# One-hot gates in bf16 with the gate cut into three parts, and one gather for both expert tables

## The chip, the cores and the metric

The kernel runs on one core of a Trainium2 chip. Its time is the device time of one execution in microseconds (us); the number given for a kernel is the median of its runs. The core has five instruction streams that run at the same time and wait for each other through semaphores: PE (the matrix engine; its weight loads are listed apart as PEld), DVE (vector), ACT (scalar), POOL (general purpose) and SP, which here only issues DMAs. ACT and POOL issue DMAs as well. Each stream runs its instructions in the order in which they were written into it.

## The reference, cut to what matters

Two layers of a mixer (an S5 state space model beside attention) followed by a PEER expert layer, for 512 tokens of width 1024. The change lies in the expert layer:

```python
def peer_ffn(h, w_q, sub_keys, u_tab, v_tab):        # h: (512, 1024); tables: (16384, 1024)
    q = (h @ w_q).reshape(tokens, 8 heads, 2, 64)
    s1, s2 = q[..., 0] @ sub_keys[:, 0], q[..., 1] @ sub_keys[:, 1]     # 128 keys each
    t1, i1 = top_k(s1, 16);  t2, i2 = top_k(s2, 16)
    best, pos = top_k(t1[:, None] + t2[None, :], 16)                    # 16 experts a head
    idx = (i1 * 128 + i2)[pos];  gate = softmax(best)                   # 128 experts a token
    act = gelu(einsum('tkd,td->tk', u_tab[idx], h))
    return einsum('tk,tkd->td', act * gate, v_tab[idx])
```

## The kernel before, in words

The tokens are four blocks of 128. For blocks 0 to 2 (384 tokens, `NT`) the expert layer is computed densely: every one of the 16384 experts is applied to every token, and a gate that is zero for the experts that were not chosen does the choosing. Block 3 is computed by gathering the rows of its chosen experts. Per layer the work goes through these stages.

**Route** (`route_block`, for blocks 3, 0, 1, 2): the top-k lists, nearly all on DVE. For block 3 it leaves `s.idx` (128 row numbers a token) and `s.gate`. For the others it transposes the two key numbers and the gate of every pick through PE into `idT` (three rows of 384 columns; a column is a token, a partition is one of its 128 picks).

**Gates** (`gates`): for each token a 128 x 128 matrix of gates (first key by second key) is made as a product of two one-hot matrices, one of them scaled by the gate. The 384 tokens go in 48 groups of 8. A group has one DVE compare of the iota row with both key rows (`L875`, tile `t8`), a scaling of the first one-hot by the gate (for two groups of three by 8 small ACT instructions, `L879`; for the third by one DVE product, `L881`; tile `small`), 8 float32 matmuls (`L885`; the trace lists each as two passes with two weight loads), and two evictions by ACT (`L887`) into a staging tile, which goes to DRAM as `gd` once in 4 groups. `t8`, `small` and the staging tile have two buffers each.

**First tables** (`u_stage`): 128 blocks of 128 experts. A block's 512 KB come in by an SP DMA (`raw`), ACT writes a rounded copy `hi` (`L166`), the remainder `lo = raw - hi` (`L167`) is made by POOL for the first 116 blocks (`NAHEAD`), and PE does 24 matmuls of 384 columns (`mm3`, `L201` to `L203`). ACT applies the gelu (`L898`) and the result goes to DRAM (`ad`). These blocks do not depend on the gates, so the scheduler puts them between the route and gate instructions as well: they are what PE does while the others route.

**Second tables** (`v_coef`, `v_block`): for each block DVE multiplies the activations by the gates (`L908`), splits the product (`L911`), and PE does 18 matmuls of 512 columns (`L921`). The last 12 blocks of the first table are done in between.

**Gather for block 3** (`gather_step`, `gather_sum`): 128 steps a layer, spread over the stages above from the route on. Step k issues from POOL's queue two indirect DMAs (`L934`), one row of `peer_u` and one of `peer_v` for each of the 128 tokens, into `ru` and `rv` (3 buffers each), and then sums step k-2: a DVE product with a row sum (`L945`, which waits for `ru`), a gelu on ACT (`L946`), a DVE product of a single column with the gate (`L947`), and a DVE multiply-add of `rv` into the output (`L948`). `issue_after(s.pace)` puts the issue behind POOL's last `lo`.

The order on each engine is set by a scheduler that works with its own estimate of durations when the kernel is built; at run time it is fixed.

## Time and profile before

| | |
|---|---|
| median of three runs | 3300.38 us (3298.41, 3300.38, 3734.48) |
| the profiled execution | 3299.41 us, span of its trace 3297.6 us |
| PE busy | 3074.1 us, 93% of the span |
| DVE busy | 2602.4 us, 79% |
| ACT busy | 1432.4 us, 43% |
| POOL busy | 1589.3 us, 48% |
| mean granted clock of PE | 0.970 |

"Busy" counts the time in which at least one instruction of the engine is listed as running. For PE an instruction's listed duration is longer than its spacing from the next, so a busy PE isn't a full one; and an instruction of DVE or POOL that has started but can't go on is still listed as busy. In time, layer 0's route runs from about 400 to 640 us, its gates from 640 to 893, the rest of its first tables to 1080, and its second tables to 1690; layer 1 has the same stages at 2040 to 2283, 2531, 2700 and 3290 us.

### The profile page before, as it was taken

To read this page: it belongs to the slowest core of one execution; us is meant where nothing else is said; L and a number is where in the kernel's file an instruction comes from. 1 tells how busy PE (TensorE), PEld (TensorE's weight loads), DVE (VectorE), ACT (ScalarE), POOL (GpSimd) and SP (SyncE) were. 2 spreads that over 40 slices of the span, in tenths; PEclk is the share of its full clock that TensorE was granted. 3 is DMA by queue.
4 is the path that set the end of the run, shared out by engine and by line. 5 is a ranking of instruction groups with operands and counts; after the bars stand their busy time and mean duration, and the time that the engine had idled before them with its cause. 6 is when DMAs were issued, how large, how long until landed. Compare 5 with 4: busy or idle time off the path is not lost. (4 is left out here: it accounts for less than half of the span.)

```text
span 3297.6 us, 45399 instructions
## 1 busy us (share of the span) xinstructions
PE 3074.1 (93%) x16178; PEld 2687.6 (82%) x16178; DVE 2602.4 (79%) x4892; ACT 1432.4 (43%) x2574; POOL 1589.3 (48%) x880
## 2 busy tenths in 40 slices
PE   8999987889999998999999999878999999999998
PEld 7757977889999776887889679878898998788887
DVE  7754799988776788898867547999886658888887
ACT  3163333478733343343333533334886333333333
POOL 3000476656688544464420004666766884544452
PEclk9999989999999999999999999889999999999999
DMA  6512376667799988999964123766777898999995
GB/s 187 188 54 64 120 253 206 210 239 268 272 310 309 326 304 288 333 331 330 338 217 121 52 71 123 249 219 196 278 256 279 302 319 315 328 352 341 340 336 213
DMA packets 391604, 811.08 MB, mean 246 GB/s; under 512 B 26928, under 2 KB 232752, under 8 KB 388304
## 3 DMA queue, kind: packets, MB, share of 16 engines
q1 hardware_dynamic: 136608, 326.23, 29.0%
q0 software_dynamic: 73728, 268.47, 23.0%
q10 hardware_dynamic: 181040, 213.48, 19.3%
q8 instruction: 127, 2.08, 0.3%
q14 instruction: 101, 0.83, 0.1%
HBM read 693.19 MB, written 114.82 MB: 245 GB/s over the span
## 5 line engine op out<-in xcount | busy, mean ns | idle before, releaser
L167 POOL TENSOR_TENSOR lo<-raw,hi 128x1024 fp32r<-128x1024 f32 x296 | 792.8, 2686 | 890.7 <-ACT hi L166 828.5
L166 ACT ACTIVATE hi<-raw 128x1024 fp32r<-128x1024 f32 x561 | 591.9, 1057 | 602.0 <-issue 157.6
L921 PE MATMUL pb<-hi,cc 128*128 128x512 f32 x2048 | 608.0, 398 | 17.7 <-DVE cc L911 11.5
L945 DVE SCALAR_TENSOR_TENSOR ru<-ru,hn 128x1024 f32<-128x1024 f32 x256 | 378.1, 1478 | 204.0 <-DMA ru<-in_peer_u_dram,idx 204.0
L921 PEld LDWEIGHTS pb<-hi,cc 128*128 128x128 f32 x2048 | 383.9, 189 | 115.2 <-DVE cc L911 16.6
L934 POOL DMA_INDIRECT rv<-in_peer_v_dram,idx x256 | 369.3, 1442 | 136.8 <-issue 45.4
L167 DVE TENSOR_TENSOR lo<-raw,hi 128x1024 fp32r<-128x1024 f32 x265 | 328.6, 1241 | 127.4 <-ACT hi L166 127.2
L934 POOL DMA_INDIRECT ru<-in_peer_u_dram,idx x256 | 377.7, 1476 | 96.1 <-DVE ru L945 33.9
L948 DVE SCALAR_TENSOR_TENSOR h<-rv,gc,h 128x1024 f32<-128x1024 f32 x256 | 404.4, 1580 | 8.2 <-DMA rv<-in_peer_v_dram,idx 5.9
L203 PE MATMUL pa<-x,lo 128*128 128x384 f32 x1120 | 387.2, 346 | 17.2 <-POOL lo L167 16.6
L201 PE MATMUL pa<-x,hi 128*128 128x384 f32 x1120 | 390.4, 349 | 12.5 <-ACT hi L166 12.5
L202 PE MATMUL pa<-x,hi 128*128 128x384 f32 x1120 | 380.1, 339 | 0.0
L201 PE MATMUL pc<-x,hi 128*128 128x384 f32 x928 | 328.4, 354 | 18.7 <-ACT hi L166 12.9
L203 PE MATMUL pc<-x,lo 128*128 128x384 f32 x928 | 325.5, 351 | 19.7 <-POOL lo L167 19.6
L921 PE MATMUL pb<-lo,cc 128*128 128x512 f32 x1024 | 324.8, 398 | 13.2 <-DVE lo L167 11.4
L921 PE MATMUL pc<-hi,cc 128*128 128x512 f32 x1024 | 323.8, 396 | 0.0
L202 PE MATMUL pc<-x,hi 128*128 128x384 f32 x928 | 320.1, 345 | 0.0
L946 ACT ACTIVATE gc<-gc 128x1 f32<-128x1 f32 x256 | 51.4, 201 | 556.5 <-DVE ru L945 506.2
L875 DVE TENSOR_TENSOR t<-io,idt 128x2048 f32<-128x2048 f32 x96 | 260.2, 2722 | 9.1 <-PE pb L885 9.1
L885 PE MATMUL pb<-small,t 128*128 128x128 f32 x1536 | 222.5, 289 | 34.2 <-ACT small L879 21.8
L910 ACT ACTIVATE cc<-c 128x384 fp32r<-128x384 f32 x256 | 133.1, 520 | 267.7 <-DVE c L908 213.1
L885 PEld LDWEIGHTS pb<-small,t 128*128 128x128 f32 x1536 | 211.6, 198 | 46.1 <-ACT small L879 30.5
(334 smaller groups left out, 5798.7 us busy)
## 6 DMA issues: line engine op xcount, KB each, us to landing
raw<-in_peer_uT_dram SPq DMA_DIRECT2D x256, 512.0 KB
raw<-in_peer_v_dram SPq DMA_DIRECT2D x256, 512.0 KB
gd<-t ACTq DMA_DIRECT2D x24, 2048.0 KB
g<-gd ACTq DMA_DIRECT2D x64, 768.0 KB
ad<-ao ACTq DMA_DIRECT2D x232, 192.0 KB
ar<-ad ACTq DMA_DIRECT2D x58, 768.0 KB
raw<-in_w_in_dram SPq DMA_DIRECT2D x34, 512.0 KB
s5p<-pE ACTq DMA_DIRECT2D x16, 512.0 KB
```

Source lines behind the costliest of these rows:

```text
L166: s.nc.scalar.activation(hi, raw, AF.Copy)
L167: ins = eng.tensor_tensor(lo, raw, hi, op=OP.subtract)
L201: mm(ps, lh, rh, start=start, stop=False)
L202: mm(ps, lh, rl, start=False, stop=False)
L203: mm(ps, ll, rh, start=False, stop=stop)
L875: v.tensor_tensor(oh, s.iota[:, None, None, :].to_broadcast([128, 2, 8, 128]), idT[:, 0:2, t0:t0 + 8, None].to_broadcast([128, 2, 8, 128]) ...
L885: nc.tensor.matmul(p[:, t], oh[:, 1, 4 * f + t], o2[:, 4 * f + t], start=True, stop=True)
L910: on_act = nc.scalar.activation(ch, c[:, 0], AF.Copy)
L921: s.nc.tensor.matmul(s.pv[tb][hf], x[:, sl], y[:, 512 * hf:512 * hf + 512], start=(first and e == 0), stop=(last and e == 2))
L934: nc.gpsimd.indirect_dma_start(out=o, out_offset=None, in_=a[n], in_offset=off)
L945: v.scalar_tensor_tensor(ru, ru, 1.0, s.hn, op0=OP.mult, op1=OP.mult, accum_out=c[:, 0:1])
L948: v.scalar_tensor_tensor(acc, rv, c[:, 2:3], acc, op0=OP.mult, op1=OP.add)
```

## The change

The one-hot matrices become bf16. `idT` is now bf16 with five rows: the two key numbers, and the gate as a sum of three bf16 parts. The 8 tokens of a group are held as 4 pairs with the pair innermost, so that neighbouring elements belong to the two tokens of a pair. DVE does two compares (`L882`) and three products (`L884`) of 1024 elements for each group, ACT no scaling; PE does three bf16 matmuls a token (`L890`), which add up in PSUM, each with a weight load. The eviction (`L892`) writes in runs of four tokens where it wrote element by element with a stride of 32. The rows of both expert tables lie behind one another in one DRAM table `peer_uv` (16384 rows of 2048 a layer): a gather step is one indirect DMA (`L939`) of 128 rows of 8 KB into one tile `ruv` (3 buffers), and the second table's blocks are read as the right halves of its rows. The gate product of a gather step moves from DVE to ACT (`L953`). Line numbers of the changed kernel differ a little: the sums `L945` and `L948` are `L951` and `L954` there.

```diff
@@ -117,7 +116,8 @@
         rel = s.t("rel", [128])
         nc.gpsimd.iota(rel, pattern=[[1, 128]], base=0, channel_multiplier=-1,
                        allow_small_or_imprecise_dtypes=True)
-        s.iota = io
+        s.iota2 = s.t("iota2", [128, 2], BF)
+        nc.vector.tensor_copy(s.iota2, io[:, :, None].to_broadcast([128, 128, 2]))
         s.ident = s.t("ident", [128])
         nc.vector.tensor_scalar(s.ident, rel, 0.0, None, op0=OP.is_equal)
         s.identb = s.t("identb", [128], BF)
@@ -856,7 +857,11 @@
             nc.tensor.transpose(p[:, 256:384], g, s.ident)
             ts = slice(b * 128, b * 128 + 128)
             v.tensor_copy(s.idT[:, 0:2, ts], p[:, 0:256].rearrange("p (a b) -> p a b", a=2))
+            rest = cut(12, 1)
             v.tensor_copy(s.idT[:, 2, ts], p[:, 256:384])
+            v.tensor_tensor(rest, p[:, 256:384], s.idT[:, 2, ts], op=OP.subtract)
+            v.tensor_copy(s.idT[:, 3, ts], rest)
+            v.tensor_tensor(s.idT[:, 4, ts], rest, s.idT[:, 3, ts], op=OP.subtract)
 
     def gates(s):
 
@@ -866,25 +871,26 @@
         idT = s.idT
         for tg in range(NT // 32):
             stg = s.t("t16", [128, 32], bufs=2)
-            gs = idT[:, 2, tg * 32:tg * 32 + 32]
             for e in range(4):
                 t0 = tg * 32 + e * 8
 
-                oh = s.t("t8", [2, 8, 128], bufs=2)
-                o2 = s.t("small", [8, 128], bufs=2)
-                v.tensor_tensor(oh, s.iota[:, None, None, :].to_broadcast([128, 2, 8, 128]),
-                                idT[:, 0:2, t0:t0 + 8, None].to_broadcast([128, 2, 8, 128]), op=OP.is_equal)
-                if GMODE[(4 * tg + e) % len(GMODE)] == "A":
-                    for t in range(8):
-                        nc.scalar.activation(o2[:, t], oh[:, 0, t], AF.Copy, scale=gs[:, 8 * e + t:8 * e + t + 1])
-                else:
-                    v.tensor_tensor(o2, oh[:, 0], gs[:, 8 * e:8 * e + 8, None].to_broadcast([128, 8, 128]), op=OP.mult)
+                oh = s.t("t8", [2, 4, 128, 2], BF, bufs=2)
+                o3 = s.t("small", [3, 4, 128, 2], BF, bufs=2)
+                col = lambda i: idT[:, i, t0:t0 + 8].rearrange("p (a t) -> p a t", t=2)[:, :, None, :] \
+                    .to_broadcast([128, 4, 128, 2])
+                for i in range(2):
+                    v.tensor_tensor(oh[:, i], s.iota2[:, None].to_broadcast([128, 4, 128, 2]), col(i), op=OP.is_equal)
+                for i in range(3):
+                    v.tensor_tensor(o3[:, i], oh[:, 0], col(2 + i), op=OP.mult)
                 for f in range(2):
                     p = s.p("pb").rearrange("p (t i) -> p t i", t=4)
                     for t in range(4):
-                        nc.tensor.matmul(p[:, t], oh[:, 1, 4 * f + t], o2[:, 4 * f + t], start=True, stop=True)
-                    o = stg[:, :, e * 8 + f * 4:e * 8 + f * 4 + 4].rearrange("p i t -> p t i")
-                    nc.scalar.activation(o, p, AF.Copy)
+                        x = 2 * f + t // 2
+                        for i in range(3):
+                            nc.tensor.matmul(p[:, t], oh[:, 1, x, :, t % 2], o3[:, i, x, :, t % 2],
+                                             start=(i == 0), stop=(i == 2))
+                    nc.scalar.activation(stg[:, :, e * 8 + f * 4:e * 8 + f * 4 + 4], p.rearrange("p t i -> p i t"),
+                                         AF.Copy)
             nc.scalar.dma_start(gd[tg], stg)
         s.gd = gd
 
@@ -927,11 +933,10 @@
         k = s.gk
         s.gk += 1
         if k < 128:
-            r = [s.ga.tile([128, D], F32, name=f"{n}{s.l}_{k}", tag=n, bufs=GLAG + 1) for n in ("ru", "rv")]
+            r = s.ga.tile([128, 2 * D], F32, name=f"ruv{s.l}_{k}", tag="ruv", bufs=GLAG + 1)
             off = bass.IndirectOffsetOnAxis(ap=s.idx[:, k:k + 1], axis=0)
             with s.tc.issue_after(getattr(s.pace, "ins", s.pace)):
-                for o, n in zip(r, ("u_flat", "v_flat")):
-                    nc.gpsimd.indirect_dma_start(out=o, out_offset=None, in_=a[n], in_offset=off)
+                nc.gpsimd.indirect_dma_start(out=r, out_offset=None, in_=a["uv_flat"], in_offset=off)
             s.grow[k] = r
         if 0 <= k - GLAG < 128:
             s.gather_sum(k - GLAG)
@@ -939,12 +944,13 @@
     def gather_sum(s, k):
         nc = s.nc
         v = nc.vector
-        ru, rv = s.grow.pop(k)
+        r = s.grow.pop(k)
+        ru, rv = r[:, 0:D], r[:, D:2 * D]
         acc = s.h[:, 3]
         c = s.ga.tile([128, 4], F32, name=f"gc{s.l}_{k}", tag="gc", bufs=4)
         v.scalar_tensor_tensor(ru, ru, 1.0, s.hn, op0=OP.mult, op1=OP.mult, accum_out=c[:, 0:1])
         nc.scalar.activation(c[:, 1:2], c[:, 0:1], AF.Gelu_apprx_tanh)
-        v.tensor_tensor(c[:, 2:3], c[:, 1:2], s.gate[:, k:k + 1], op=OP.mult)
+        nc.scalar.activation(c[:, 2:3], c[:, 1:2], AF.Copy, scale=s.gate[:, k:k + 1])
         v.scalar_tensor_tensor(acc, rv, c[:, 2:3], acc, op0=OP.mult, op1=OP.add)
 
     def peer(s, prep_next):
@@ -955,7 +961,7 @@
         s.hn = s.k("hn", [D])
         s.idx = s.t("idx", [128], I32)
         s.gate = s.t("gate", [128])
-        uT, vt = a["peer_uT"][l], a["peer_v"][l]
+        uT, vt = a["peer_uT"][l], a["peer_uv"][l, :, D:2 * D]
         uspec = lambda b: (uT[b].rearrange("p k e -> p (k e)"), [8, 128], b < NAHEAD)
         vspec = lambda b: (vt[128 * b:128 * b + 128], [1024], b % 4 == 0)
         M = NAHEAD
@@ -969,7 +975,7 @@
             order.append(("v", M + i))
         specs = [uspec(b) for b in range(M)] + [(uspec if kd == "u" else vspec)(b) for kd, b in order]
         with s.phase("one"):
-            gb = s.ga.tile([128, D], F32, name=f"gb{l}", tag="ru", bufs=GLAG + 1)
+            gb = s.ga.tile([128, D], F32, name=f"gb{l}", tag="ruv", bufs=GLAG + 1)
             xn = s.norm_T(a["norm2_g"], gb, "t8", "pa")
             nc.gpsimd.tensor_copy(s.hn, xn)
             s.route()
@@ -1109,18 +1115,16 @@
-    o["peer_u"] = c(f("peer_u"))
     o["peer_uT"] = c(f("peer_u").reshape(L, 128, 128, 8, 128).transpose(0, 1, 4, 3, 2))
+    o["peer_uv"] = np.concatenate([f("peer_u"), f("peer_v")], axis=2)
-    if "peer_u" in a:
-        a["u_flat"] = a["peer_u"].rearrange("l e d -> (l e) d")
+    if "peer_uv" in a:
+        a["uv_flat"] = a["peer_uv"].rearrange("l e d -> (l e) d")
```

On DVE in the gates stage of layer 0, a little after its start. Before (`t` is `t8`, 128x2048 is one compare for a group, `h` the output of block 3):

```order
L875 TENSOR_TENSOR t_567_3624<-io_65,idt_2743 128x2048
L881 TENSOR_TENSOR small_3625<-t_567_3624,idt_2743 128x1024
L875 TENSOR_TENSOR t_571_3640<-io_65,idt_2743 128x2048
L945 SCALAR_TENSOR_TENSOR ru_25_6527,gc_25_6685<-ru_25_6527,hn_2185 128x1024
L875 TENSOR_TENSOR t_575_3663<-io_65,idt_2743 128x2048
L947 TENSOR_TENSOR gc_25_6685<-gc_25_6685,gate_2187 128x1
L875 TENSOR_TENSOR t_580_3688<-io_65,idt_2743 128x2048
L948 SCALAR_TENSOR_TENSOR h_60<-rv_25_6528,gc_25_6685,h_60 128x1024
```

On DVE at the same place of the changed kernel:

```order
L882 TENSOR_TENSOR t_568_3702<-iota_4_69,idt_2745 128x1024 x2
L951 SCALAR_TENSOR_TENSOR ruv_25_7176,gc_25_7328<-ruv_25_7176,hn_2187 128x1024
L884 TENSOR_TENSOR small_3703<-t_568_3702,idt_2745 128x1024 x3
L954 SCALAR_TENSOR_TENSOR h_60<-ruv_25_7176,gc_25_7328,h_60 128x1024
L882 TENSOR_TENSOR t_572_3737<-iota_4_69,idt_2745 128x1024 x2
L884 TENSOR_TENSOR small_3738<-t_572_3737,idt_2745 128x1024 x3
```

Five products or compares of 1024 elements stand where one of 2048 stood (with a product of 1024 in each third group), the single-column product is gone, and gather sums come once in about three groups as before (17 multiply-adds of gather steps lie inside the stage in either order).

On POOL in the same stage. Before:

```order
L167 TENSOR_TENSOR lo_7618<-raw_7538,hi_7617 128x1024
L167 TENSOR_TENSOR lo_7652<-raw_7572,hi_7651 128x1024
L934 DMA ru_40_7682<-in_peer_u_dram,idx_2186 128x1024
L934 DMA rv_40_7683<-in_peer_v_dram,idx_2186 128x1024
L167 TENSOR_TENSOR lo_7695<-raw_7615,hi_7694 128x1024
```

On POOL in the changed kernel:

```order
L167 TENSOR_TENSOR lo_7596<-raw_7518,hi_7595 128x1024
L939 DMA ruv_31_7626<-in_peer_uv_dram,idx_2188 128x2048
L167 TENSOR_TENSOR lo_7637<-raw_7559,hi_7636 128x1024
L167 TENSOR_TENSOR lo_7671<-raw_7593,hi_7670 128x1024
L939 DMA ruv_32_7701<-in_peer_uv_dram,idx_2188 128x2048
```

One issue stands where two stood, still one step for two `lo`. On PE the order of the first-table matmuls among the gate matmuls changes little: between the first and the last gate matmul of layer 0 stood 740 of them and now stand 702 (1168 and 1176 ahead of the stage, 905 and 935 behind it, up to the first second-table matmul); in layer 1 it was 748 and is 754.

## Rows read from the trace of the kernel before

**Rows 1.** Stages: length; busy PE, PEld, DVE, ACT, POOL; clock; DMA share; GB/s.

```profile
640.00:893.00 253.00, 232.90 (x1523) 226.28 (x1524) 211.69 (x132) 205.38 (x422) 151.48 (x64) 0.97 0.68 244
...
1080.00:1690.00 610.00, 580.63 (x2553) 470.54 (x2552) 520.78 (x888) 233.11 (x392) 291.87 (x171) 0.99 0.90 313
...
2283.00:2531.00 248.00, 229.79 (x1520) 224.58 (x1520) 209.43 (x130) 205.62 (x420) 164.67 (x64) 0.97 0.71 253
```

**Rows 2.** Groups of DVE, layer 0's gates stage (640 to 893 us).

```profile
L875 DVE TENSOR_TENSOR t<-io,idt 128x2048 f32<-128x2048 f32 x47 | 125.7, 2688 | 3.7 <-PE pb L885 3.7
L948 DVE SCALAR_TENSOR_TENSOR h<-rv,gc,h 128x1024 f32<-128x1024 f32 x17 | 32.5, 1910 | 0.3
L945 DVE SCALAR_TENSOR_TENSOR ru<-ru,hn 128x1024 f32<-128x1024 f32 x16 | 29.0, 1812 | 30.4 <-DMA ru<-in_peer_u_dram,idx 30.4
L881 DVE TENSOR_TENSOR small<-t,idt 128x1024 f32<-128x1024 f32 x16 | 19.5, 1221 | 0.1
L947 DVE TENSOR_TENSOR gc<-gc,gate 128x1 f32<-128x1 f32 x17 | 10.1, 592 | 5.1 <-ACT gc L946 4.9
```

**Rows 3.** Lines by source: shortest, median and longest duration in ns.

```profile
L875 DVE TENSOR_TENSOR t<-io,idt x96: 2276/2283/5414, 630.5 to 2524.2; 128x2048 f32<-128x2048 f32 x96
L945 DVE SCALAR_TENSOR_TENSOR ru<-ru,hn x256: 1196/1218/4550, 426.3 to 3262.9; 128x1024 f32<-128x1024 f32 x128
L947 DVE TENSOR_TENSOR gc<-gc,gate x256: 131/152/5332, 429.3 to 3265.7; 128x1 f32<-128x1 f32 x128
L948 DVE SCALAR_TENSOR_TENSOR h<-rv,gc,h x256: 1226/1279/6346, 435.5 to 3266.9; 128x1024 f32<-128x1024 f32 x128
L167 POOL TENSOR_TENSOR lo<-raw,hi x296: 2347/2416/5558, 346.2 to 3260.0; 128x1024 fp32r<-128x1024 f32 x148
```

**Rows 4.** Timeline of DVE around 708 us.

```profile
708.67 4.55 DVE L945 SCALAR_TENSOR_TENSOR ru<-ru,hn 128x1024 f32<-128x1024 f32 x1 [2.12 <-DMA ru<-in_peer_u_dram,idx]
```

**Rows 5.** Timeline of POOL around the same time.

```profile
705.49 1.87 POOL L934 DMA_INDIRECT rv<-in_peer_v_dram,idx  x1 [0.30 <-issue]
707.39 4.74 POOL L167 TENSOR_TENSOR lo<-raw,hi 128x1024 fp32r<-128x1024 f32 x2
```

**Rows 6.** Groups of POOL, layer 0's gates stage.

```profile
L167 POOL TENSOR_TENSOR lo<-raw,hi 128x1024 fp32r<-128x1024 f32 x32 | 91.9, 2873 | 94.3 <-ACT hi L166 89.0 <-ACT gc L946 5.0
```

**Rows 7.** DVE's bf16 sums in the route stage (512, 1024 and 2048 elements).

```profile
L833 DVE TENSOR_TENSOR t<-t x24: 409/688/3197, 400.2 to 2281.0; 128x2048 bf16<-128x2048 bf16 x8, 128x1024 bf16<-128x1024 bf16 x8, 128x512 bf16<-128x512 bf16 x8
```

**Rows 8.** Timeline of DVE at 1201 us: neighbours without a wait.

```profile
1200.01 1.27 DVE L948 SCALAR_TENSOR_TENSOR h<-rv,gc,h 128x1024 f32<-128x1024 f32 x1
1201.20 0.55 DVE L908 TENSOR_TENSOR c<-ar,g 128x384 f32<-128x384 f32 x1
```

**Rows 9.** Waits of DVE for a gather, layer 0's gates stage, then layer 1's.

```profile
DVE ru L945 <- DMA ru<-in_peer_u_dram,idx: 30.4, 12, 6.1
...
DVE ru L945 <- DMA ru<-in_peer_u_dram,idx: 27.4, 8, 5.8
```

**Rows 10.** Timeline of PE around 701 us, nine spacings.

```profile
700.11 0.34 PE L201 MATMUL pc<-x,hi 128*128 128x384 f32 x1
...
701.69 0.34 PE L201 MATMUL pc<-x,hi 128*128 128x384 f32 x1
```

**Rows 11.** Timeline of PE around 717 us.

```profile
716.84 2.02 PE L885 MATMUL pb<-small,t 128*128 128x128 f32 x16 [1.05 <-DVE small L881]
718.62 0.42 PE L202 MATMUL pc<-x,hi 128*128 128x384 f32 x1
```

**Rows 12.** Groups of ACT, layer 0's gates stage.

```profile
L887 ACT ACTIVATE t<-pb 128x512 f32<-128x512 f32 x96 | 98.0, 1116 | 2.7 <-issue 1.4 <-ACT gc L946 0.5 <-PE pa L203 0.4
L879 ACT ACTIVATE small<-t,idt 128x128 f32<-128x128 f32 x248 | 76.0, 391 | 35.6 <-DVE t L875 28.7 <-PE pb L885 6.9
```

**Rows 13.** ACT's plain eviction of 512 elements in the route stage, by source.

```profile
L776 ACT ACTIVATE t<-pb x32: 578/597/618, 357.8 to 2212.5; 128x512 f32<-128x512 f32 x32
```

**Rows 14.** Waits of the whole span: who for whom, us, times, longest.

```profile
DVE gc L947 <- ACT gc L946: 53.4, 51, 9.6
```

More of the change, by code (lines that the diff above doesn't have):

```diff
@@ L31 @@
 PF = 4
-GMODE = "AAV"
 GA = 58
@@ L757, in route @@
             s.evac(qT[:, hd], p)
-        s.idT = s.t("idt", [3, NT])
+        s.idT = s.t("idt", [5, NT], BF)
         for b in (3, 0, 1, 2):
@@ L1111, in layout @@
     o["keys"] = c(f("peer_keys").transpose(0, 2, 4, 1, 3).reshape(L, 128, 8, 128))
-    o["peer_u"] = c(f("peer_u"))
     o["peer_uT"] = c(f("peer_u").reshape(L, 128, 128, 8, 128).transpose(0, 1, 4, 3, 2))
-    o["peer_v"] = c(f("peer_v"))
+    o["peer_uv"] = np.concatenate([f("peer_u"), f("peer_v")], axis=2)
     o["norm_f"] = c(f("norm_f"))
@@ L1120, in views @@
     a = dict(a)
-    if "peer_u" in a:
-        a["u_flat"] = a["peer_u"].rearrange("l e d -> (l e) d")
-        a["v_flat"] = a["peer_v"].rearrange("l e d -> (l e) d")
+    if "peer_uv" in a:
+        a["uv_flat"] = a["peer_uv"].rearrange("l e d -> (l e) d")
     return a
```

## The prediction

> **What bounds the kernel now.** I read the busy times by stage first, since the change touches one stage above all, the gates: 253 us in layer 0 and 248 in layer 1 [rows 1]. There PE, DVE, ACT and POOL are busy for 233, 212, 205 and 151 us, and none fills the stage. In the second tables PE is busy for 581 of 610 us [rows 1], so what DVE or ACT save there buys little.
>
> For the gates I then read DVE's groups [rows 2] against the median of each line over the whole run [rows 3]. Each group runs longer inside the stage than its median: a compare (`L875`) 2.688 us against 2.283, a multiply-add (`L948`) 1.910 against 1.279. Something holds DVE while it is listed as busy. The timeline names it: at 708.67 a sum (`L945`) lasts 4.55 us where 1.218 is usual, and ends at 713.22 [rows 3, 4]; POOL's two `lo` run from 707.39 to 712.13 [rows 5], so that the sum ends 1.09 us after them. It did almost all of its work once they were over: a `lo` and a DVE instruction with two operands in SBUF exclude each other. The sum had done about 0.13 us at the hand-over (1.218 - 1.09), so a `lo`, 2.416 us by its median [rows 3], costs DVE about 2.29 us.
>
> The account of layer 0's stage is then: DVE's own work, counts of [rows 2] by medians of [rows 3] and `L881`'s 1.221: 47 x 2.283 + 17 x 1.279 + 16 x 1.218 + 16 x 1.221 + 17 x 0.152 = 170.6 us. Neighbours overlap by 0.08 us (1200.01 + 1.27 against 1201.20 [rows 8]), so 113 instructions need 9 less; the stage's 19 other instructions are tiny, some 2 us. That leaves 164. The 32 `lo` [rows 6] take 32 x 2.29 = 73. Together 237 of 253 us; 16 are left, in which DVE waits with no `lo` running. Layer 1 has two DVE instructions fewer [rows 1]: about 163 + 73 = 236 of 248, 12 left. So **DVE and POOL's `lo`, which take turns, set the stage**. DVE's waits for gathered rows, 30.4 us in 12 waits and 27.4 in 8 [rows 9], lie partly under those turns.
>
> PE could do it faster: first-table matmuls are spaced (701.69 - 700.11)/9 = 0.175 us [rows 10], gate passes (718.62 - 716.84)/16 = 0.111 [rows 11]; 740 and 768 of them are 130 + 85 = 215 us. ACT's 205 us hold 76.0 of scalings and 98.0 of evictions [rows 12].
>
> **The change part by part.** *DVE in the gates.* Out go a 2.283 compare per group and a 1.221 product in each third: 48 and 16 in a layer, 109.6 + 19.5 = 129, less 64 x 0.08 of overlap, 124. In come five bf16 instructions of 1024 elements per group, 240 in a layer. The nearest row is the bf16 sum of the route stage, eight each of 512, 1024 and 2048, whose median, 0.688, is the 1024 one [rows 7]; less the overlap, 0.61. 240 x 0.61 = 146. So DVE gets **22 us more** work per layer, not less. The lower bound is half of `L881`'s net 1.14, 0.57: 10 us less. `L947` leaves DVE: 17 x (0.152 - 0.08) = 1 us. DVE's own work becomes 185 and 184 us.
>
> A `lo` comes with 24 first-table matmuls, and by the order between the first and the last gate matmul stand 702 of them in layer 0 and 754 in layer 1: 29.25 and 31.4 `lo`, by 2.29 us 67 and 72. So 185 + 67 = 252 and 184 + 72 = 256, where 237 and 236 stood. What is left over, 16 and 12 us, holds waits for ACT and PE that the change shortens; I keep about half, 7 and 5: **259 and 261 us, +6 and +13**. With nothing left over the stages are 252 and 256, with the 0.57 price 242 and 246; with all of it left 268 and 268. In layer 0 some 30 first-table matmuls (905 behind the stage, now 935) go where PE sets the pace: 30 x 0.175 = **+5**. The term is **+24**, between -8 and +40.
>
> [...]
>
> *PE in the gates.* Two float32 passes a token become three bf16 ones, 1152 in a layer instead of 768. No row has a bf16 pass of this size; bounded by half of the float32 spacing (0.056) and all of it (0.111) they take 64 to 128 us, beside 702 x 0.175 = 123 or 754 x 0.175 = 132. I take the middle, 96: PE needs 219 and 228, below 259 and 261. At the upper bound it needs 251 and 260, as much as DVE and POOL: then the two limits meet, which the range's upper part covers.
>
> *ACT in the gates.* 76.0 us of scalings go [rows 12]. The eviction takes 1.116 now and 0.597 where it writes plainly [rows 12, 13]; the new pattern lies between, or, as a bound, stays. ACT falls to 79 to 129 us plus a few for `L953`. POOL's `lo` waits 89.0 us for ACT's `hi` [rows 6]; these waits shrink, but the number of `lo` is set by PE's consumption and each still stops DVE, so I count nothing.
>
> *The joint gather.* POOL issues once where it issued twice, 1.87 us the issue [rows 5]. This could let the next rows land earlier by up to that: 20 waits in the two stages [rows 9] by 1.87 is -37 us. Against it, the sum waited for 512 KB of `peer_u` and now waits for the whole 1 MB tile: another 512 KB at the stage's 244 GB/s [rows 1] is 2.15 us, in 20 waits +43. Behind a waiting sum all gate compares of DVE are queued, and PE and ACT behind them. The step has two steps' time to land (`GLAG`), and the same bytes go through the same queue; I take **0**, between -37 and +43.
>
> *Elsewhere.* `L947` leaves DVE, 222 more times: 222 x 0.07 = 16 us, and its waits for ACT (53.4 in the run [rows 14]) move to the multiply-add, behind one more ACT instruction in the same chain. Where PE sets the end this is hidden; I take half, -8. Of the waits I take 10% as gained, -5, since DVE may now put other work between sum and multiply-add. The route gains three small DVE instructions for each of three blocks, 18 in all, between `L947`'s 0.152 and the 0.55 of 384 elements [rows 3, 8]; at 0.28 that is +5. The reads of the second table keep their size and rows, spaced wider: nothing, hidden by the prefetch; if that cover went, PE's stage of 610 us would show it. The term is **-8**, between -30 and +10.
>
> **The sum.** The profiled execution took 3299.41 us, within 1 us of the median 3300.38, so the two are one. 3299 + 24 + 0 - 8 = **3315 us**.
>
> **The rivals.** *Faster: the turns of DVE and `lo` cease to bind.* If ACT's late `hi` is what makes `lo` collide with DVE, or if the halved bf16 traffic lets `lo` pass, PE sets the gates, 219 and 228 us: -34 and -20, so 3299 - 54 + 5 - 8 = 3242, and 3226 if a gate pass takes 0.076 us. For it speak the 89.0 us that `lo` waits for ACT [rows 6]; against it that the 2.29 us price holds for each `lo` whenever it comes. I give it 0.10.
>
> *Slower: the joint gather comes late.* If the second half of the rows delays not only the 20 waits but every sum of both stages (32, 16 a stage), 32 x 2.15 = +69: 3384. It decides from 1.6 us a step on, where the total passes 2%. For it: DVE already waits for 20 of these 32 [rows 9], so there is no slack on those, and a landed `ru` no longer suffices. Against it: the total bytes are the same, and rv of step k came before ru of step k+1 in the queue anyway. 0.12.
>
> *Much slower: the bf16 products run at the float32 rate.* [Rows 7] show the fast rate for contiguous operands only; here one operand repeats a pair of values 128 times. At `L881`'s net 1.14, 240 x (1.14 - 0.61) = 127 us a layer: 3569. A broadcast of single elements would be a weightier reason than one of pairs; 0.08.
>
> [...]
>
> **How the numbers follow.** The forecast has 0.70, the rivals 0.10, 0.12 and 0.08. Its terms' ends (-32, +16; -37, +43; -22, +18 from the values taken) don't all fall together; as the root of the squares they give -54 and +49: 3261 to 3364 for the forecast alone. The range takes in the slower rival, 3384, and leaves out the faster one and the float32 rate, 0.18 together: **3260 to 3385**. About 2%, 66 us, is what a measurement of this kernel can tell from no change; the borders are 3234 and 3366. Below 3234 lie half of the faster rival and a tail of the forecast of 0.04: 0.09. Above 3366 lie most of the joint gather's case (0.08), the float32 rate (0.08) and a tail (0.02): 0.18. Within: 0.73.
>
> **What the changed profile would show.** Right: gates stages of 255 to 268 us, `L882` and `L884` at 0.61 to 0.69 us where nothing holds them and longer where a `lo` runs; ACT below 135 us in the stage, DVE's and `lo`'s sum still within 15 us of the stage; the gather's waits as before. Stages of 215 to 230 with PE full mean the faster rival; waits at `L951` that grew by 1.5 us or more each mean the joint gather; `L884` at 1.1 us or more means the float32 rate. What would make all of it wrong is a change outside the gates: a longer second-table stage from the joint table's rows, or a route stage that DVE no longer sets.

## The result and the profile after

The changed kernel takes **3313.87 us** (median of 13 runs), the one before 3298.41 (13 runs beside it); the ratio of their times is 1.0055, with a 95% interval of 1.0043 to 1.0067. The ratio leaves out the one slow run before, of 3734.48 us. The kernel is slower by half a per cent: sure, and small. The profiled execution of the changed kernel took 3313.1 us.

First the busy times by stage, of the kernel before and then of the changed one, cut here at the first compare and the last matmul of the gates and the first and last matmul of the second tables (columns as in [rows 1]).

```profile
630.50:890.90 260.40, 230.83 (x1511) 224.18 (x1511) 220.71 (x140) 208.97 (x433) 153.41 (x63) 0.96 0.67 240
890.90:1059.60 168.70, 162.68 (x907) 161.35 (x907) 117.06 (x86) 59.89 (x99) 141.37 (x77) 0.97 0.92 314
1059.60:1695.70 636.10, 606.73 (x2665) 491.60 (x2664) 538.76 (x911) 242.68 (x406) 301.23 (x178) 0.99 0.89 311
2272.50:2530.90 258.40, 230.69 (x1525) 225.16 (x1524) 219.83 (x140) 210.93 (x433) 169.22 (x65) 0.96 0.70 250
2530.90:2698.50 167.60, 160.14 (x897) 159.14 (x896) 92.53 (x85) 59.59 (x98) 140.82 (x74) 0.98 0.90 302
2698.50:3287.60 589.10, 585.88 (x2570) 478.08 (x2569) 490.05 (x645) 220.36 (x353) 272.09 (x170) 1.00 0.91 322
```

```profile
626.30:895.00 268.70, 220.88 (x1868) 197.62 (x1867) 256.84 (x303) 105.95 (x194) 130.95 (x47) 0.91 0.63 230
895.00:1067.90 172.90, 166.79 (x940) 165.19 (x938) 89.65 (x64) 62.70 (x116) 122.27 (x59) 0.99 0.89 307
1067.90:1686.80 618.90, 603.42 (x2664) 490.78 (x2663) 540.26 (x844) 259.42 (x478) 203.98 (x107) 0.99 0.90 319
2259.60:2547.20 287.60, 230.73 (x1920) 207.55 (x1918) 256.82 (x306) 110.19 (x199) 134.59 (x51) 0.91 0.62 227
2547.20:2707.60 160.40, 158.52 (x903) 157.58 (x900) 83.27 (x61) 61.31 (x113) 117.64 (x56) 1.00 0.90 316
2707.60:3301.00 593.40, 587.18 (x2569) 478.86 (x2568) 483.26 (x577) 240.12 (x425) 174.76 (x99) 1.00 0.90 320
```

Read the lengths pairwise. The gates grew by 8 us in layer 0 and 29 in layer 1; the rest of the first tables by 4 and -7; the second tables by -17 and 4; what lies ahead of each gates stage shrank by 4 and 4 (630.5 against 626.3; 1695.7 to 2272.5 against 1686.8 to 2259.6). That makes the 13 us between the two spans. In the gates DVE rose from 221 to 257 busy us and fills the stage of layer 0 but for 12; ACT fell from 209 to 106.

DVE's groups in layer 0's gates stage after, to be set against [rows 2], and one line's shortest, median and longest duration against [rows 3]:

```profile
L884 DVE TENSOR_TENSOR small<-t,idt 128x1024 bf16<-128x1024 bf16 x144 | 117.0, 865 | 0.0
L882 DVE TENSOR_TENSOR t<-iota,idt 128x1024 bf16<-128x1024 bf16 x96 | 89.1, 967 | 3.3 <-PE pb L890 3.2
L951 DVE SCALAR_TENSOR_TENSOR ruv<-ruv,hn 128x1024 f32<-128x1024 f32 x18 | 28.3, 1570 | 6.3 <-DMA ruv<-in_peer_uv_dram,idx 6.3
L954 DVE SCALAR_TENSOR_TENSOR h<-ruv,gc,h 128x1024 f32<-128x1024 f32 x17 | 28.0, 1648 | 0.6 <-ACT gc L953 0.6
```

```profile
L882 DVE TENSOR_TENSOR t<-iota,idt x192: 674/681/2891, 626.3 to 2540.7; 128x1024 bf16<-128x1024 bf16 x192
```

A compare takes 0.681 us where nothing holds it and 0.967 on average in the stage: it still takes turns with POOL's `lo`. The timeline shows both sides. First DVE, then POOL, around 706 us (`x3` merges three instructions into one row):

```profile
703.04 1.89 DVE L884 TENSOR_TENSOR small<-t,idt 128x1024 bf16<-128x1024 bf16 x3
704.85 1.28 DVE L954 SCALAR_TENSOR_TENSOR h<-ruv,gc,h 128x1024 f32<-128x1024 f32 x1
706.05 1.29 DVE L882 TENSOR_TENSOR t<-iota,idt 128x1024 bf16<-128x1024 bf16 x2
707.25 1.89 DVE L884 TENSOR_TENSOR small<-t,idt 128x1024 bf16<-128x1024 bf16 x3
709.52 3.05 DVE L882 TENSOR_TENSOR t<-iota,idt 128x1024 bf16<-128x1024 bf16 x2 [0.38 <-PE pb L890]
```

```profile
705.42 6.00 POOL L167 TENSOR_TENSOR lo<-raw,hi 128x1024 fp32r<-128x1024 f32 x1 [10.18 <-ACT hi L166]
711.56 1.24 POOL L939 DMA_INDIRECT ruv<-in_peer_uv_dram,idx  x1
```

The three products from 703.04 to 704.85 make 0.603 us each. Here the `lo` is the one that waits: it takes 6.00 us instead of 2.4 while DVE runs one instruction behind the other, until DVE stops for PE for 0.38 us; and the gather's issue stands behind it. In layer 1 the same thing comes back to DVE (POOL, then DVE):

```profile
2308.89 9.41 POOL L167 TENSOR_TENSOR lo<-raw,hi 128x1024 fp32r<-128x1024 f32 x1 [5.38 <-ACT hi L166]
2318.45 1.24 POOL L939 DMA_INDIRECT ruv<-in_peer_uv_dram,idx  x1
```

```profile
2316.77 2.69 DVE L882 TENSOR_TENSOR t<-iota,idt 128x1024 bf16<-128x1024 bf16 x2 [0.73 <-PE pb L890]
2329.62 1.23 DVE L951 SCALAR_TENSOR_TENSOR ruv<-ruv,hn 128x1024 f32<-128x1024 f32 x1 [10.16 <-DMA ruv<-in_peer_uv_dram,idx]
```

The `lo` took 9.41 us, the issue came at 2318.45, the rows at 2329.6, and DVE stood still for 10.16 us. DVE's waits for rows after, layer 0's gates and then layer 1's, against [rows 9]:

```profile
DVE ruv L951 <- DMA ruv<-in_peer_uv_dram,idx: 6.3, 3, 5.0
...
DVE ruv L951 <- DMA ruv<-in_peer_uv_dram,idx: 22.6, 4, 10.2
```

And of PE and ACT in layer 0's gates, a run of gate passes (44 from 699.92 to 702.98: 0.070 us each) and the eviction's group (the granted clock is 0.50 when the run of passes begins and 1.00 from 701.1 on; the passes are 0.107 us apart before that and 0.057 after, so the 0.070 is a mixture):

```profile
699.92 3.25 PE L890 MATMUL pb<-small,t 128*128 128x128 bf16 x44
702.98 0.42 PE L201 MATMUL pc<-x,hi 128*128 128x384 f32 x1
```

```profile
L892 ACT ACTIVATE t<-pb 128x512 f32<-128x512 f32 x95 | 54.6, 594 | 63.6 <-PE pb L890 62.9 <-ACT gc L952 0.6
```

### The profile page after: what moved, and what is told of

Its sections match the earlier page's. It is cut to its first block, busy times and chain, and to the rows that moved or that the text cites. A ratio compares the mean times of both kernels' runs of the same rounds, so it can differ in the third digit from the quotient of the medians.

```text
span 3311.1 us, 45952 instructions
## 1 busy us (share of the span) xinstructions
PE 3064.0 (93%) x16946; PEld 2646.1 (80%) x16946; DVE 2626.0 (79%) x5007; ACT 1279.5 (39%) x2316; POOL 1238.6 (37%) x624
## 5 line engine op out<-in xcount | busy, mean ns | idle before, releaser
L167 POOL TENSOR_TENSOR lo<-raw,hi 128x1024 fp32r<-128x1024 f32 x296 | 830.6, 2810 | 1202.9 <-ACT hi L166 1055.6
L951 DVE SCALAR_TENSOR_TENSOR ruv<-ruv,hn 128x1024 f32<-128x1024 f32 x256 | 352.4, 1377 | 168.0 <-DMA ruv<-in_peer_uv_dram,idx 167.1
L954 DVE SCALAR_TENSOR_TENSOR h<-ruv,gc,h 128x1024 f32<-128x1024 f32 x256 | 420.9, 1644 | 78.8 <-ACT gc L953 76.3
L927 PEld LDWEIGHTS pb<-hi,cc 128*128 128x128 f32 x2048 | 383.5, 189 | 113.4 <-ACT cc L916 16.7
L939 POOL DMA_INDIRECT ruv<-in_peer_uv_dram,idx x256 | 358.6, 1401 | 287.1 <-DVE h L954 195.7
L203 PE MATMUL pa<-x,lo 128*128 128x384 f32 x1120 | 390.6, 349 | 19.5 <-POOL lo L167 19.4
L201 PE MATMUL pc<-x,hi 128*128 128x384 f32 x928 | 331.8, 358 | 2.1 <-ACT hi L166 2.0
L202 PE MATMUL pc<-x,hi 128*128 128x384 f32 x928 | 323.9, 349 | 0.0
L890 PE MATMUL pb<-small,t 128*128 128x128 bf16 x2304 | 182.2, 225 | 80.8 <-DVE small L884 80.5
L890 PEld LDWEIGHTS <-t 128*128 128x128 bf16 x2304 | 140.0, 100 | 125.9 <-DVE small L884 85.7
L927 PEld LDWEIGHTS pb<-lo,cc 128*128 128x128 f32 x1024 | 192.3, 189 | 55.7 <-DVE lo L167 9.4
L884 DVE TENSOR_TENSOR small<-t,idt 128x1024 bf16<-128x1024 bf16 x288 | 235.9, 871 | 0.1
L203 PEld LDWEIGHTS pa<-x,lo 128*128 128x128 f32 x1120 | 215.7, 193 | 24.8 <-POOL lo L167 23.9
```

What stands on the lines that cost most here:

```text
L167: ins = eng.tensor_tensor(lo, raw, hi, op=OP.subtract)
L201: mm(ps, lh, rh, start=start, stop=False)
L202: mm(ps, lh, rl, start=False, stop=False)
L203: mm(ps, ll, rh, start=False, stop=stop)
L884: v.tensor_tensor(o3[:, i], oh[:, 0], col(2 + i), op=OP.mult)
L890: nc.tensor.matmul(p[:, t], oh[:, 1, x, :, t % 2], o3[:, i, x, :, t % 2], start=(i == 0), stop=(i == 2))
```

## The experiments

The theory: in the gates DVE's own work and POOL's `lo` take turns and set the end; the change gives DVE more of it, and the joint gather is worth little. The rivals: the joint gather's late rows cost the time, or PE or ACT sets the gates.

**Each half alone.** `gates_only` is the changed kernel with the gather of before; `joint_only` is the kernel before with the new gather step. Their edits are the two halves of the diff above; the lines that matter, for `gates_only` against the changed kernel (`joint_only` has them the other way round against the kernel before):

```diff
-            r = s.ga.tile([128, 2 * D], F32, name=f"ruv{s.l}_{k}", tag="ruv", bufs=GLAG + 1)
+            r = [s.ga.tile([128, D], F32, name=f"{n}{s.l}_{k}", tag=n, bufs=GLAG + 1) for n in ("ru", "rv")]
-        nc.scalar.activation(c[:, 2:3], c[:, 1:2], AF.Copy, scale=s.gate[:, k:k + 1])
+        v.tensor_tensor(c[:, 2:3], c[:, 1:2], s.gate[:, k:k + 1], op=OP.mult)
```

> The bf16 gates alone: two gathers a step and the gate product on DVE as before. Theory of turns (DVE's own work and POOL's lo take turns and set the gates; the joint gather is worth about nothing): about 3314 + 8 = 3322 us, between 3308 and 3335, gates stages of 265 to 290 us. Rival (the joint gather's late rows cost what was lost, 22.6 us of waits in layer 1's gates among it): about 3290 us, and the DVE waits for rows in the two gates stages below 10 us.

> The joint gather and the gate product on ACT alone, with the old float32 gates. Theory of turns: 3298 - 8 = 3290 us, between 3275 and 3303, gates stages of 255 to 262 us as before. Rival (joint gather late): 3310 to 3320 us, with gates stages longer by what DVE waits more for the rows.

Measured: `gates_only` 3318.43 us, ratio to before 1.008 (1.005 to 1.0109); `joint_only` 3286.43, ratio 0.9976 (0.9959 to 0.9994), with before at 3293.96 beside them. Over all runs the gates cost 24 us, and the rest gives 8 back. The rival of the late rows falls: with the old gather DVE's waits for rows are as short, 2.5 us in layer 0's gates and still 16.7 in layer 1's:

```profile
DVE ru L951 <- DMA ru<-in_peer_u_dram,idx: 2.5, 2, 1.5
...
DVE ru L951 <- DMA ru<-in_peer_u_dram,idx: 16.7, 3, 10.0
```

By stage the halves are less clean. The gates stages of `gates_only`, then of `joint_only`, in one profiled execution each:

```profile
629.50:893.80 264.30, 213.71 (x1868) 190.70 (x1869) 258.76 (x319) 100.61 (x174) 119.32 (x62) 0.95 0.64 233
2280.90:2550.50 269.60, 216.25 (x1851) 193.22 (x1852) 250.66 (x319) 99.43 (x172) 133.47 (x60) 0.92 0.62 226
623.50:888.40 264.90, 236.43 (x1519) 225.88 (x1517) 235.10 (x124) 214.52 (x450) 127.42 (x49) 0.97 0.65 239
2250.00:2521.00 271.00, 237.41 (x1523) 231.26 (x1522) 225.65 (x124) 212.79 (x451) 129.91 (x49) 0.93 0.64 234
```

Against 260 and 258 us before, each half lengthens the two stages together by some 15 to 17 us. For `joint_only` I had expected them as before, 255 to 262: that missed. It is not the waits for rows, 19.5 and 26.3 us there against 30.4 and 27.4; DVE is held longer in its instructions, in layer 0 a compare 3.019 us where it was 2.680:

```profile
L875 DVE TENSOR_TENSOR t<-io,idt 128x2048 f32<-128x2048 f32 x48 | 143.9, 3019 | 1.1 <-PE pb L885 1.1
```

Why, no run shows. Outside the gates `joint_only` is 7 us shorter ahead of each gates stage and 11 in layer 0's second tables, and 11 longer in layer 1's. Its profiled run, 3300.66 us, was the slowest of ten and shows no gain in sum, so these sizes are rough, and where the 8 us of the median lie is open.

**Less work for DVE.** `parts2` leaves out the third part of the gate in the products and matmuls.

```diff
-                for i in range(3):
+                for i in range(2):
                     v.tensor_tensor(o3[:, i], oh[:, 0], col(2 + i), op=OP.mult)
...
-                        for i in range(3):
+                        for i in range(2):
...
-                                             start=(i == 0), stop=(i == 2))
+                                             start=(i == 0), stop=(i == 1))
```

> The gate's third part is left out of the products and of the matmuls (its value is still computed in the route), so gates are less exact. It takes 48 products of 0.602 us off DVE in each layer. Theory of turns: 96 x 0.602 = 58 us less if all of it is on the path; taken as 50, about 3264 us, gates stages some 25 us shorter each. Rival (PE, ACT or the gather sets the gates): within 10 us of the changed kernel's 3314.

Measured: 3249.53 us, ratio 0.9869 (0.9835 to 0.9903). That is 64 us under the changed kernel for 58 us of DVE work. The edit takes a third of the gate passes off PE too, so by itself it doesn't tell DVE from PE; the next pair of runs does. The gates are 236 us long in both layers:

```profile
630.80:867.00 236.20, 197.58 (x1521) 181.06 (x1521) 222.99 (x256) 104.11 (x197) 119.44 (x49) 0.91 0.73 269
2229.40:2465.40 236.00, 194.17 (x1502) 175.83 (x1501) 227.01 (x253) 103.47 (x194) 126.18 (x49) 0.93 0.74 265
```

**The `lo` on the other engine.** `lo_dve` lets DVE make the `lo` of the blocks that run in the gates; `before_lo_dve` does the same to the kernel before.

```diff
-        uspec = lambda b: (uT[b].rearrange("p k e -> p (k e)"), [8, 128], b < NAHEAD)
+        uspec = lambda b: (uT[b].rearrange("p k e -> p (k e)"), [8, 128], b < NAHEAD and not 49 <= b < 79)
```

> Blocks 49 to 78 of the first table, those that run in the gates stage, have their lo made by DVE in place of POOL; the scheduler then puts 968 and 977 first-table matmuls inside the stages where 702 and 754 stood. Theory of turns: a lo costs DVE 1.14 us when DVE makes it and about 2.3 when POOL does, so some 30 lo a layer save 1.1 us each, and PE gets more of its work done in the stage: 60 to 100 us less, about 3235 us. Rival (DVE is bound by its own instructions and POOL's lo run mostly in its idle time): 34 us more work on DVE in each gates stage, and 3300 to 3350 us.

> The kernel before with the lo of blocks 49 to 78 made by DVE, as in lo_dve; 947 and 926 first-table matmuls then stand inside the gates stages. Theory of turns: the same gain per lo, about 1 us, but ACT with its 205 us of scalings, evictions and hi comes next, so less than lo_dve gained: about 3240 us, between 3215 and 3265. Rival (only the changed kernel suffers from POOL's lo): no gain, 3290 to 3300 us. If it comes out at 3207 like lo_dve, the bf16 gates are worth nothing even where ACT could be the limit.

Measured: `lo_dve` 3206.84 us, ratio 0.9732 (0.97 to 0.9764), and `before_lo_dve` 3233.64, ratio 0.983 (0.9793 to 0.9867). With `lo_dve` DVE has 30 more instructions of 1.2 us in the stage, and the kernel is 107 us faster than the changed one. DVE's groups of `lo_dve` in layer 0's gates, and the stage's busy times:

```profile
L884 DVE TENSOR_TENSOR small<-t,idt 128x1024 bf16<-128x1024 bf16 x144 | 99.6, 744 | 0.0
L882 DVE TENSOR_TENSOR t<-iota,idt 128x1024 bf16<-128x1024 bf16 x96 | 75.1, 822 | 5.4 <-PE pb L890 5.4
L167 DVE TENSOR_TENSOR lo<-raw,hi 128x1024 fp32r<-128x1024 f32 x30 | 36.5, 1216 | 0.0
```

```profile
625.30:901.30 276.00, 255.12 (x2138) 236.39 (x2138) 262.00 (x350) 124.40 (x227) 91.76 (x34) 0.96 0.74 276
```

The compares and products are held less (0.822 and 0.744 us against 0.967 and 0.865), with 13 `lo` left on POOL there where 32 were. The stage is not shorter, 276 us against 268.7, but 984 first-table matmuls lie in it where 714 did, and the rest of the first tables takes 122 us instead of 173. PE thus did 270 matmuls more in 7 us more: it was not what bound the stage. In the kernel before the rival falls too (it suffers from POOL's `lo` as well); but what comes next there is PE, busy 259 of 271 us, not ACT as I expected:

```profile
626.20:897.60 271.40, 259.44 (x1725) 256.50 (x1724) 235.61 (x187) 222.44 (x453) 110.67 (x52) 0.99 0.75 274
```

**The `lo` of the route as well.** The same edit with `b < 4 or 79 <= b < NAHEAD`, on the changed kernel (`lo_dve_route`) and on the one before (`before_lo_route`).

> The lo of blocks 4 to 78 made by DVE, those that run during the route stage as well as those of the gates stage, POOL from 79 on. 2212 and 2918 first-table matmuls then stand ahead of the gates stage, 706 and 701 in it. Theory of turns: in the route too a POOL lo costs DVE more (71 us of held time for 41 lo, 1.7 each) than one made by DVE (1.14): some 25 us a layer of DVE time beside what lo_dve saves, and 3180 to 3230 us. Rival (the route is bound by DVE's own work, and POOL's lo cost it little): 41 x 1.14 = 47 us a layer more on DVE there, 3250 to 3300 us.

> The kernel before with the lo of blocks 4 to 78 made by DVE, as in lo_dve_route. It tells whether the bf16 gates still pay with the lo placed best: lo_dve_route gained 9 us over lo_dve. Theory (without POOL's lo in the stage PE and ACT bound the old gates, and the bf16 gates relieve both): about 3225 us, between 3205 and 3245, behind lo_dve_route's 3197 by some 25 us. Rival (DVE alone is the limit everywhere, and the old gates need 20 us less of it): 3190 us or less.

Measured: `lo_dve_route` 3197.54 us, ratio 0.9713 (0.9683 to 0.9743), and `before_lo_route` 3187.43, ratio 0.9674 (0.9633 to 0.9715). The first came as expected. The second did not: the old gates are not 25 us behind there but level or ahead, as the rival said. So the 27 us by which `lo_dve` beats `before_lo_dve` is no law of the bf16 gates; with other blocks on DVE the order turns round, and the intervals overlap. Why the one pair differs and the other doesn't I didn't settle. By stage, the old gates take 245 and 242 us in `before_lo_route`, the new ones 252 and 255 in `lo_dve_route`: there the bf16 gates are the longer ones.

**ACT's share.** `old_evict` writes the eviction with the old stride.

```diff
-                    nc.scalar.activation(stg[:, :, e * 8 + f * 4:e * 8 + f * 4 + 4], p.rearrange("p t i -> p i t"),
-                                         AF.Copy)
+                    o = stg[:, :, e * 8 + f * 4:e * 8 + f * 4 + 4].rearrange("p i t -> p t i")
+                    nc.scalar.activation(o, p, AF.Copy)
```

> The changed kernel with the eviction written with its stride of 32 as before: ACT gets about 0.52 us more for each of 192 evictions, 100 us in the run. Theory of turns (ACT waits for PE and DVE in the gates): within 10 us of 3314. Rival (ACT's relief is what paid for the longer DVE work): 30 to 50 us slower, 3345 to 3365.

Measured: 3312.44 us, ratio 1.0051 (1.0029 to 1.0074), the same as the changed kernel's, though each eviction takes 1.122 us instead of 0.597:

```profile
L893 ACT ACTIVATE t<-pb x192: 1027/1122/1212, 641.9 to 2543.9; 128x512 f32<-128x512 f32 x192
```

100 us of ACT are worth nothing here. This gives back the eviction's share of ACT's relief; the scalings' share was not tested.

**The pairs.** `unpaired` holds the tokens one by one (the lines that matter; the iota row and the matmuls' indices follow).

```diff
-                oh = s.t("t8", [2, 4, 128, 2], BF, bufs=2)
-                o3 = s.t("small", [3, 4, 128, 2], BF, bufs=2)
-                col = lambda i: idT[:, i, t0:t0 + 8].rearrange("p (a t) -> p a t", t=2)[:, :, None, :] \
-                    .to_broadcast([128, 4, 128, 2])
+                oh = s.t("t8", [2, 8, 128], BF, bufs=2)
+                o3 = s.t("small", [3, 8, 128], BF, bufs=2)
+                col = lambda i: idT[:, i, t0:t0 + 8, None].to_broadcast([128, 8, 128])
```

> The changed kernel with tokens not in pairs: key and gate are broadcast along the innermost 128 elements, all operands still bf16. Theory (the fast rate hangs on the pair): each of the 480 products and compares takes 1.14 to 1.22 us instead of 0.68, DVE gets 127 us more in each layer, the scheduler puts 1613 and 1637 first-table matmuls into the stage; 3420 to 3570 us. Rival (bf16 alone brings the rate): 0.68 us each and within 60 us of 3314.

Measured: 3487.93 us (two runs), ratio 1.0594 (1.0557 to 1.0632), and 1.212 us for each compare or product:

```profile
L881 DVE TENSOR_TENSOR t<-iota,idt x192: 1208/1212/3428, 623.4 to 2859.7; 128x1024 bf16<-128x1024 bf16 x192
```

All operands have two bytes in both kernels; the pair alone brings the time from 1.212 to 0.681 us.

**The issue behind the `lo`.** `no_pace` takes away the rule that orders a gather's issue behind POOL's last `lo`.

```diff
-            with s.tc.issue_after(getattr(s.pace, "ins", s.pace)):
-                nc.gpsimd.indirect_dma_start(out=r, out_offset=None, in_=a["uv_flat"], in_offset=off)
+            nc.gpsimd.indirect_dma_start(out=r, out_offset=None, in_=a["uv_flat"], in_offset=off)
```

> The changed kernel without the rule that puts a gather's issue behind POOL's last lo; POOL's order changes little. Theory (rows come late in the gates because a lo that waits for DVE holds up the issue queued behind it): the waits of DVE for rows in the two gates stages, 6.3 and 22.6 us, fall below 15 together, and the time by 5 to 20 us, to about 3302. Rival (the rows are late because 1 MB takes long to land, or the order on POOL is what counts and stays): the waits stay at 25 us or more and the time within 5 us of 3314.

Measured: 3402.33 us, ratio 1.0338 (1.03 to 1.0376). Both theories missed. The waits for rows did vanish (none is listed in either gates stage), but the scheduler moved gather steps forward: 32 and 31 sums stand in the two stages where 18 and 19 did, and they take DVE's time. The groups of layer 0's stage:

```profile
L884 DVE TENSOR_TENSOR small<-t,idt 128x1024 bf16<-128x1024 bf16 x144 | 125.4, 922 | 0.0
L953 DVE SCALAR_TENSOR_TENSOR h<-ruv,gc,h 128x1024 f32<-128x1024 f32 x31 | 53.1, 1713 | 0.0
L950 DVE SCALAR_TENSOR_TENSOR ruv<-ruv,hn 128x1024 f32<-128x1024 f32 x32 | 44.0, 1378 | 0.0
```

The stage is 312 us long instead of 269: 14 steps of two instructions at 1.2 us are 34 of these 43, and it holds 39 `lo` where it held 32. The run moved two things and settles nothing on the 10 us wait of layer 1. A fourth row buffer, which might take that wait away by itself, wasn't tried.

**Both levers.** `parts2_route` joins `parts2` and `lo_dve_route` (the gate's third part is left out).

> Both at once: lo of blocks 4 to 78 on DVE, and the gate's third part left out of products and matmuls as in parts2. Theory of turns (DVE is still the limit of the gates once POOL's lo are gone): 96 products of 0.60 us less, some 45 to 60 us under lo_dve_route, about 3145. Rival (PE has become the limit there, busy 231 of 252 us): less than 25 us gained, 3172 or more.

Measured: 3167.64 us, ratio 0.9617 (0.9579 to 0.9656), 30 us under `lo_dve_route`, between the two: the missing third part still shortens the gates by 30 us a layer (252 to 222 in layer 0), but half of it is lost elsewhere, 15 us in the second tables of layer 0 alone (638 instead of 623). It takes work off DVE and off PE, and the run doesn't tell which of the two counts here. It is the fastest kernel measured, at the price of a less exact gate; with the full gate it is `before_lo_route`, which has the gates and the gather of before.

## Why the prediction was right

The mechanism of the gates holds: DVE gets more work, and DVE and `lo` together set the stage (`lo_dve`). The sum (3315, measured 3313.87) is closer than its parts, and that is luck. Over all runs the two halves came to +24 (`gates_only`) and -8 (`joint_only`), as the two terms had it, but with intervals of some 10 and 6 us to either side. In the profiled pair the gates with the rest of the first tables grew by 34 us, where the term was +24, and all else fell by 21, where it was -8: two errors that cancel. Step by step:

- **DVE's new work**, 0.61 us an instruction: 0.603. Right; the rival of the float32 rate is what `unpaired` shows, and it is the pairs that keep it away (a compare takes 0.681 us with them, 1.212 without).
- **The price of a `lo`**, 2.29 us for each. After, the time by which the four groups of DVE above exceed their medians (0.680 for a product, 0.681 for a compare, 1.219 and 1.279 for the sums) is 26.6 + 27.5 + 6.3 + 6.3 = 67 us, the number that I had, but from other factors: 32 `lo` of 2.1 us, where I had 29.25 of 2.29. Their number did not fall (32 before, 32 after, between the first compare and the last matmul); I had counted it by the clock before and by the order after. Before, the price was wrong: there the same excess, (2.688 - 2.283) x 47 + (1.910 - 1.279) x 17 + (1.812 - 1.218) x 16 + (0.592 - 0.152) x 17, is only 47 us, 1.5 a `lo`, where the account put 73. (I also read every group as held; `L881` is not, 1.221 us in the stage and 1.222 over the run.) The difference lay under DVE's 41 us of idle time. So "237 of 253, 16 left over" was mis-sized: it was about 211 and 41.
- **What is left over**, 16 and 12, of which I kept 7 and 5: by the cut of the tables above, DVE's own work in layer 0 rose by 16 us, the time in which it is held by 20, and its idle time fell by 28, from 40 to 12. So the sum of +8 came about otherwise than forecast: I had the `lo` cost 6 us less, and the idle time pay 9. That +6 is near it is luck.
- **The two stages**, +6 and +13: +8 and +29. Layer 1 is off most. It has 31 us of idle time (287.6 - 256.82), 22.6 of them waits for rows in four sums. I had not thought of a `lo` that waits for DVE and holds up the gather behind it on POOL: the issue for each of the four stands right behind a `lo` of 3.9 to 9.4 us. Half of the excess is no loss to the kernel: layer 1's rest of the first tables is 7 us shorter.
- **First-table matmuls pushed behind layer 0's stage**, +5: the rest grew by 4.2.
- **The joint gather**, 0 between -37 and +43: `joint_only` gives -8 in all, together with the gate product. Both ends of the range were waits for rows. These fell from 57.8 to 28.9 us in the two stages, with the new gates alone to 19.2 and with the joint gather alone to 45.8: mostly the longer DVE work covers them. That the joint gather would leave the gates stages as they were is not so, in its one profile they are 17 us longer with it alone.
- **PE**: a gate pass takes 0.070 us on average in the run above, below the 0.083 taken; PE waits for `L884` (35 us in layer 0), as an engine that isn't the limit would. The stage's granted clock fell from 0.96 to 0.91, since part of the time it was 0.50 where it was else 1.00 (from 697.7 to 701.1, for instance; PE had stood waiting for 2.65 us ahead of 696.45, but what moves the clock no run shows). PE has the slack: in `lo_dve` it did 270 matmuls more in 7 us more.
- **ACT**: 106 us in the stage, forecast below 135, and `old_evict` shows that the eviction's part of its relief is worth nothing.
- **Elsewhere**, -8: second tables -17 and +4, the stretches ahead of the gates -4 and -4. In sum -21 in the one profiled pair, of which 14 lie in PE's idle time in layer 0's second tables (29 us before, 15 after); `joint_only` gives -8 over all runs, and I take that. What shortened this stage isn't shown: over the thirteen profiles it takes 618 to 642 us, and `before_lo_dve`, with the old gates and the old gather, has it at 618. Of the parts of the term one went the other way: the waits of the chain for ACT rose from 53.4 [rows 14] to 76.3 us in the run, where I had counted a tenth of them as gained.
- **The signs**: `L882` and `L884` at 0.68 us and ACT below 135 came. Layer 0's stage, 268.7 us, is at the border of what I had named, layer 1's, 287.6, beyond it, with 31 us of idle time instead of at most 15; and the waits for rows were not as before but half.

The turns are seen in the held compares (0.967 us in layer 0's stage against 0.681, with bf16 operands) and in the 107 us that `lo_dve` gained by giving DVE more instructions. Not every instruction of DVE is held: in the kernel before, all 128 of the route's `L787`, which reads one tile, took 0.265 to 0.295 us, though a `lo` ran beside 60 of them for over half of their time, while `L911`, which reads two, took up to 3.036 us where its median is 0.551; `L881`, which reads two as well, took 1.229 at most, its median being 1.222. What makes the one wait and the other not, no run shows.

## What to carry to other kernels

Where a trace shows that instructions of two engines hold each other up, count the other engine's as work of the first: in layer 0 of the changed kernel each subtraction on POOL cost DVE 2.1 us (67 us over 32 of them) where DVE itself needs 1.2, so that moving 30 of them in each layer onto the busy engine gained 3%. A relief for an engine that waits was worth nothing here (100 us of ACT, 3312.44 us without it against 3313.87), and the bf16 rewrite was more work: five instructions of 0.60 us a group where one of 2.28 stood, and a product of 1.22 in each third group. When an account of a stage leaves idle time over, ask how much of the other engine's time lies hidden in it, before the change fills it. And a sum that comes out to the microsecond says little of its terms: look at each stage.

## What I had not expected of the hardware

The turns of DVE and POOL are uneven. Of the 66 `lo` in the two gates stages after, 45 took 2.3 to 3 us, but eight took 5 to 11.1 us: DVE ran up to thirteen instructions back to back before POOL got its turn. The traces show where the long waits end. All 15 `lo` of 3.8 us or more got their turn only at a break in DVE's stream: seven where DVE paused, if only for 0.02 us (0.73 us in the case of 2308.89), and eight right behind the accumulator read that follows a sum. So the longest, the `lo` that begins at 2338.54 and takes 11.1 us, ends 2.2 us after this read; on DVE:

```profile
2346.18 1.22 DVE L951 SCALAR_TENSOR_TENSOR ruv<-ruv,hn 128x1024 f32<-128x1024 f32 x1
2347.32 0.08 DVE L951 DVE_READ_ACCUMULATOR ruv<-ruv,hn 128x1 f32 x1
2347.32 2.87 DVE L884 TENSOR_TENSOR small<-t,idt 128x1024 bf16<-128x1024 bf16 x1
```

Most of the short ones got their turn between two DVE instructions without a pause. What decides which way it goes the runs don't show.

`no_pace` made the waits for rows vanish and the kernel 88 us slower, with some 13 gather sums more in each gates stage: a wait in the profile says little of what its removal brings.
